# Row sums of the adaLN blocks: one group of matmuls for up to four blocks

## The chip, the cores and the metric

The kernel runs on one core of a Trainium2 chip. Its engines work side by side, each through its own list of instructions: TensorE (PE, with its weight loads as PEld) multiplies matrices, VectorE (DVE), ScalarE (ACT) and GpSimd (POOL) work on elements, and SyncE (SP) issues the DMA transfers. SBUF is the working memory, PSUM holds what TensorE writes, in eight banks. The metric is the device time of one execution in microseconds. The kernel before took 2109.31 us in the median of 3 runs (2108.45 to 2116.08).

## The reference

A backbone of two layers works on 256 latent and 256 context tokens of 1024 features. Each layer is a feed-forward part, a token mixing of four branches, and a second feed-forward part. Before each of them the tokens are normalised, scaled and shifted, and its result is gated. These nine vectors of a layer come from the conditioning alone:

```python
mod = [m[:, None, :] for m in jnp.split(jax.nn.silu(c) @ w_ada[l] + b_ada[l], N_MOD, axis=-1)]
mod_c = jnp.split(jax.nn.silu(c_ctx) @ w_ada[l] + b_ada[l], N_MOD, axis=-1)

def ffn_half(z, shift, scale, gate, norm, wg, wu, wd):
    return z + 0.5 * gate * swiglu(modulate(rmsnorm(z, norm), shift, scale), wg, wu, wd)
```

`w_ada[l]` has 1024 rows and 9 x 1024 columns. There are only two rows of conditioning (c and c_ctx), so this product is a very thin one: two output rows, 9216 columns, for each layer.

## The kernel before

**The main stream.** The tokens lie in SBUF with features on the 128 partitions. Every large product is made with split operands: a weight unit of 128 x 1024 is brought in (`raw`), ScalarE rounds it to `whi` (line 81), VectorE takes the rest as `wlo` (line 84), and TensorE makes three matmuls of 512 columns for each of 8 steps (lines 110 to 112): 24 products to a unit. In a feed-forward part the units come in pairs, `pg` (gate) and `pu` (up), then the down products `pd`, and for the last two chunks `last`. Their results go through three PSUM banks in turn (`mm`); four further banks are for small things and one, `ada`, for the work of this change. The weights have four buffers for `whi` and four for `wlo`, so ScalarE and VectorE work up to four units ahead.

**The adaLN blocks.** The thin product is cut into 18 blocks of 512 columns for each layer. The first four blocks of layer 0 are made on TensorE at the cold start (`ada_pe`, line 263, 32 columns of weights in each of four column tiles). The other 14 of layer 0 and all 18 of layer 1 are worked off beside the feed-forward stream by a generator, `ada` (line 274). For a block, VectorE multiplies each of the four pieces of weights (512 KB each) with the conditioning and adds them into two accumulators `aacc` (lines 283 and 285), one for c and one for c_ctx. At the end of a block the 128 partitions have to be summed: two copies on ScalarE and two additions on VectorE fold both accumulators into one tile `afold`, its upper half for c and its lower half for c_ctx (lines 292 to 295). Then TensorE sums the rows of each half: the weights are `pick`, 128 x 32, with a one in column 0 or 1, and four matmuls of 128 columns go to four column tiles, that is to four groups of 32 partitions of the bank (line 297). `ada_done` reads the bank with one 32 x 32-wise transpose (line 250, tile `adat`) and adds the biases in two small additions (line 253), whose results stand in `mod`.

**What sets the order.** `pump` advances the generator by one step; `unit` calls it after each weight unit, at a rate. A block has four steps, with one piece of weights each. `mods` pumps until the values that a stage needs are there. At the end of a feed-forward part (`f == 1`) the open block is finished before the last chunks begin, in layer 0's first part and layer 1's first part all that are left. The engines' lists are made from this code by a scheduler, which keeps TensorE's work in the order of the code and may move element work a little.

The names that the prediction uses: `afold` (the folded block), `ada` (its PSUM bank), `adat` and `mod` (its read-out), `whi`/`wlo` (weights), `pg`, `pu`, `pd` (PSUM results), `sg` (the Silu of `pg`, line 535).

Of the kernel before, what the change touches and what calls it, by code (L numbers as in the profile page):

```python
# [10 lines left out]
F32 = mybir.dt.float32  # L11
# [6 lines left out]
P = 128  # L18
# [4 lines left out]
TT = 2 * T  # L23
# [9 lines left out]

RATE_FIRST, RATE_NEXT = 1.0, 0.62


O_AQ, O_AK, O_AV, O_BQ, O_BF, O_BB, O_BI, O_BG, O_C, O_DQ, O_DK, O_DV, O_G = (
    0, 256, 384, 512, 768, 1024, 1280, 1536, 1792, 2048, 2304, 2560, 2816)
# [20 lines left out]
class Net:  # L59
    def __init__(self, ctx, tc, ins, out):  # L60
        self.ctx, self.tc, self.nc, self.i, self.out = ctx, tc, tc.nc, ins, out
        self.n = 0
        pool = lambda name, **kw: ctx.enter_context(tc.tile_pool(name=name, **kw))
        self.cp = pool("const", bufs=1)
        self.wp = pool("weights", bufs=4)
        self.tp = pool("temps", bufs=2)
        self.ps = pool("psum", bufs=1, space=bass.MemoryType.PSUM)
        self.fill = self.apool = None
        self.steady, self.due = False, 0.0


# [197 lines left out]
    def ada(self, l, first):  # L269


        nc = self.nc
        for s in range(first, 18):
            self.within = True
            acc = [self.apool.tile([P, 512], F32, tag=f"aacc{r}", name="aacc") for r in range(2)]
            for k2 in range(NK // 2):
                w = self.ada_load(l, s, k2)
                for j in range(2):
                    k = 2 * k2 + j
                    for r in range(2):  # L280
                        c = self.sil[:, k, r:r + 1]
                        if k == 0:
                            nc.vector.tensor_scalar(out=acc[r], in0=w[:, j], scalar1=c, scalar2=None, op0=ALU.mult)
                        else:
                            nc.vector.scalar_tensor_tensor(out=acc[r], in0=w[:, j], scalar=c, in1=acc[r],  # L285
                                                           op0=ALU.mult, op1=ALU.add)
                if k2 < NK // 2 - 1:
                    yield True
            ps = self.ps.tile([P, TT], F32, tag="ada", bufs=1, name="ada")

            t = self.apool.tile([P, 512], F32, tag="afold", name="afold")
            nc.scalar.copy(t[:64], acc[0][64:])
            nc.scalar.copy(t[64:], acc[1][:64])
            nc.vector.tensor_tensor(out=t[:64], in0=t[:64], in1=acc[0][:64], op=ALU.add)
            nc.vector.tensor_tensor(out=t[64:], in0=t[64:], in1=acc[1][64:], op=ALU.add)
            for g in range(4):
                nc.tensor.matmul(ps[32 * g:32 * g + 32, :P], self.pick, t[:, g * P:(g + 1) * P], start=True, stop=True,
                                 tile_position=(0, 32 * g))
            self.ada_done(l, s, ps)
            self.within = False  # L300
            yield True

    def mods(self, l, j):
        while not set(range(j * NK, (j + 1) * NK)) <= self.have[l]:
            assert self.fill
            self.pump()
        return self.mod[l][:, j * NK:(j + 1) * NK]

    def gain(self, l, j, col):
# [162 lines left out]
    def cold_units(self, wgu, hp, evac, off):  # L472
# [32 lines left out]
        for _ in ada(0):  # L505
            pass
        self.keep_warm(8)
        ws = [self.unit(wgu[u // 2, u % 2]) for u in range(4)]
        aw += [loads(j) for j in range(1, 4)]
        steps = chain.from_iterable(ada(j) for j in range(1, 4))  # L510
        for item in COLD:
            if item == "a":
# [8 lines left out]
        return hh, hl  # L521

    def ffn(self, l, wgu, wd, col, mods, segs, rate=0, whole=False, cold=False):

        nc, tc = self.nc, self.tc
        n = T * len(segs)
        gate = None
        off = self.place(l, col)
        with tc.tile_pool(name=f"ffn{col}_{l}", bufs=1) as hp:
            hp.tile([P, LINE // 2], F32, name="pad")  # L530
            self.apool, self.rate = hp, rate
            def evac(pg, pu, hh, hl, c, c0, c1):
                w = c1 - c0
                s = hp.tile([P, TT], F32, tag="sg", bufs=2, name="sg")
                nc.scalar.activation(s[:, :w], pg[:, :w], AF.Silu)
                nc.vector.tensor_tensor(out=s[:, :w], in0=s[:, :w], in1=pu[:, :w], op=ALU.mult)
                self.split(s[:, :w], hh[:, c, c0:c1], hl[:, c, c0:c1])

            for f in range(2):
                c = 0  # L540
                if cold and f == 0:
                    hh, hl = self.cold_units(wgu[l], hp, evac, off)
                    c = 2
                    self.steady = True
                else:
                    hh, hl = self.hidden(hp, off)
                while c < FH:
                    if f == 0 and c == 0:
                        def first(r, j0, pss):
                            for j in range(0, len(pss), 2):  # L550
                                evac(pss[j], pss[j + 1], hh, hl, c + (j0 + j) // 2, *HALF[r])

                        ws = [self.unit(wgu[l, c + j // 2, j % 2]) for j in range(4)]
                        if len(segs) == 1:
                            self.early_units(ws, l, hp, hh, hl)
                        else:
                            self.first_units(ws, l, col, mods[0], mods[1], segs, lambda r: (
                                [self.mm(), self.mm(), self.mm(), self.aux()] if r == 0 else
                                [self.aux(), self.aux(), self.mm(), self.mm()]), first, 2)
                        c += 2  # L560
                        self.steady = True
                        continue
                    pg, pu = self.mm("pg"), self.mm("pu")
                    pool = hp if f == 0 and c == 2 else None
                    for j, p in ((0, pg), (1, pu)):
                        self.mm3(p[:, :n], self.unit(wgu[l, f * FH + c, j], NK * P, pool), self.xh, self.xl, range(NK), 0, n)
                    evac(pg, pu, hh, hl, c, 0, n)
                    c += 1
                if gate is None:
                    gate = self.gate(l, mods[2])  # L570
                if f == 1:
                    self.fresh(segs)

                def down(m, ps, c0, c1, mid=iter(()), ws=[None] * NK):
                    if ws[m] is None:
                        pool = hp if f == 1 and m >= NK - 2 else None
                        ws[m] = (self.unit(wd[l, f, m, :, :6 * P], 6 * P, pool),
                                 self.unit(wd[l, f, m, :, 6 * P:], (FH - 6) * P, pool))
                    self.mm3(ps, ws[m][0], hh, hl, range(6), c0, c1, last=False)
                    next(mid, None)  # L580
                    self.mm3(ps, ws[m][1], hh, hl, range(6, 9), c0, c1, first=False, last=False)
                    next(mid, None)
                    self.mm3(ps, ws[m][1], hh, hl, range(9, FH), c0, c1, first=False, k0=3)

                for m in range(NK - 2 * f):
                    ps = self.mm("pd")
                    down(m, ps[:, :n], 0, n)
                    for r in segs:
                        self.update(ps, m, gate, r, r * T, f == 1)
                if f == 1:  # L590
                    while self.fill and (whole or self.within):
                        self.pump()
                    self.steady = False
                    self.last_chunks(down, gate, segs)

# [659 lines left out]
```

## Time and profile before

| | us |
|---|---|
| median of 3 runs | 2109.31 |
| lowest and highest | 2108.45, 2116.08 |
| the profiled execution | 2115.61 |
| its span, first to last instruction | 2113.8 |
| TensorE busy in it | 2087.5 (99%) |
| VectorE busy | 1434.9 (68%) |
| ScalarE busy | 904.5 (43%) |

The span is the profiled execution from its first to its last instruction; 1.8 us lie around it. A busy share is an average over stages. Matmuls overlap one another, and their ends are modelled, so a matmul's duration is not what it costs: that is read from the starts of the instructions before and after it. TensorE's granted clock is at its upper level, 2.4 GHz, in all slices of the page.

### The profile page before, as it was taken

How to read it: one execution, taken by the hardware profiler on the slowest of the kernel's cores; microseconds unless marked ns; L12 is line 12 of the kernel's file. 1: busy time of each engine (PE TensorE's matmuls, PEld its weight loads, DVE VectorE, ACT ScalarE, POOL GpSimd, SP SyncE). 2: the span in 40 equal slices, each digit the busy share in tenths (PEclk: the TensorE clock that was granted, in tenths of full speed). 3: DMA queues.
4: the chain of work that ended last, by engine and by line, in shares of the span. 5: the costliest groups of instructions: out<-in, count | busy, mean ns of one | idle time of the engine just before them, and what ended most of it. 6: DMA issues, size and time to landing. Idle time of an engine off the chain costs nothing.

```text
span 2113.8 us, 31650 instructions
## 1 busy us (share of the span) xinstructions
PE 2087.5 (99%) x12446; PEld 1801.0 (85%) x12446; DVE 1434.9 (68%) x2355; ACT 904.5 (43%) x1488; POOL 39.4 (2%) x95
## 2 busy tenths in 40 slices
PE   8999999999999999999999999999999999999998
PEld 5888888988888888988888898888889989999998
DVE  5988986676366455676676667667666858677555
ACT  3332333547446433433233343223335655666443
POOL 0000000001000000000000000000000000000000
PEclk9999999999999999999999999999999999999999
DMA  7655654221222222344454334345443233455553
GB/s 304 216 175 188 215 186 140 96 98 51 75 76 80 71 97 98 110 143 138 144 183 157 124 128 161 130 156 173 146 128 114 98 120 110 141 184 181 176 189 116
DMA packets 89509, 296.71 MB, mean 140 GB/s; under 512 B 10256, under 2 KB 12176, under 8 KB 89360
## 3 DMA queue, kind: packets, MB, share of 16 engines
q1 hardware_dynamic: 89360, 294.69, 41.4%
q8 instruction: 98, 1.61, 0.3%
q14 instruction: 51, 0.42, 0.1%
HBM read 293.60 MB, written 1.05 MB: 139 GB/s over the span
## 4 chain that ended last, share of the span: by engine, by line
PE 94%; DVE 2%; ACT 2%; issue 1%; DMA 0%; DVEq 0%; ACTq 0%; SPq 0%
PE pg L110 6%; PE pu L110 6%; PE pg L112 6%; PE pu L112 6%; PE pg L111 6%; PE pu L111 6%; PE pd L110 6%; PE pd L112 6%; PE pd L111 6%; PE gate L112 4%; PE gate L110 4%; PE gate L111 4%; PE proj L111 2%; PE proj L110 2%; PE proj L112 2%; PE blev L777 2%
## 5 line engine op out<-in xcount | busy, mean ns | idle before, releaser
L81 ACT CAST whi<-raw 128x1024 fp32r<-128x1024 f32 (+2 forms) x444 | 430.7, 972 | 827.4 <-PE pu L111 200.3
L84 DVE TENSOR_TENSOR wlo<-raw,whi 128x1024 fp32r<-128x1024 f32 (+2 forms) x444 | 498.2, 1123 | 289.3 <-ACT whi L81 282.5
L285 DVE SCALAR_TENSOR_TENSOR aacc<-araw,sil,aacc 128x512 f32<-128x512 f32 x448 | 312.5, 745 | 122.0 <-DMA araw<-in_wada 121.6
L112 PE MATMUL pg<-xs,wlo 128*128 128x512 f32 (+1 forms) x640 | 233.0, 364 | 0.0
L112 PE MATMUL pu<-xs,wlo 128*128 128x512 f32 (+1 forms) x640 | 233.0, 364 | 0.0
L110 PE MATMUL pg<-xs,whi 128*128 128x512 f32 (+1 forms) x640 | 232.5, 363 | 0.4 <-ACT xs L376 0.4
L110 PE MATMUL pu<-xs,whi 128*128 128x512 f32 (+1 forms) x640 | 232.3, 363 | 0.0
L111 PE MATMUL pg<-xs,whi 128*128 128x512 f32 (+1 forms) x640 | 231.4, 362 | 0.0
L111 PE MATMUL pu<-xs,whi 128*128 128x512 f32 (+1 forms) x640 | 231.3, 361 | 0.0
L112 PE MATMUL pd<-hh,wlo 128*128 128x512 f32 (+1 forms) x616 | 224.3, 364 | 0.0
L110 PE MATMUL pd<-hh,whi 128*128 128x512 f32 (+1 forms) x616 | 223.8, 363 | 0.0
L111 PE MATMUL pd<-hl,whi 128*128 128x512 f32 (+1 forms) x616 | 222.7, 361 | 0.0
L110 PE MATMUL gate<-xs,whi 128*128 128x512 f32 (+1 forms) x512 | 172.5, 337 | 0.0
L112 PE MATMUL gate<-xs,wlo 128*128 128x512 f32 (+1 forms) x512 | 171.7, 335 | 0.0
L111 PE MATMUL gate<-xs,whi 128*128 128x512 f32 (+1 forms) x512 | 170.8, 334 | 0.0
L110 PEld LDWEIGHTS pg<-xs,whi 128*128 128x128 f32 x640 | 120.8, 189 | 20.8 <-issue 1.8
L110 PEld LDWEIGHTS pu<-xs,whi 128*128 128x128 f32 x640 | 120.8, 189 | 20.1 <-issue 2.0
L111 PEld LDWEIGHTS pu<-xs,whi 128*128 128x128 f32 x640 | 120.2, 188 | 19.4
L111 PEld LDWEIGHTS pg<-xs,whi 128*128 128x128 f32 x640 | 120.2, 188 | 19.4
L112 PEld LDWEIGHTS pg<-xs,wlo 128*128 128x128 f32 x640 | 120.1, 188 | 18.5
L112 PEld LDWEIGHTS pu<-xs,wlo 128*128 128x128 f32 x640 | 120.1, 188 | 18.5
L110 PEld LDWEIGHTS pd<-hh,whi 128*128 128x128 f32 x616 | 116.2, 189 | 19.5 <-issue 2.2
(278 smaller groups left out, 3794.5 us busy)
## 6 DMA issues: line engine op xcount, KB each, us to landing
raw<-in_wgu SPq DMA_DIRECT2D x176, 512.0 KB, 4.0
araw<-in_wada SPq DMA_DIRECT2D x128, 512.0 KB, 3.3
raw<-in_wgate SPq DMA_DIRECT2D x64, 512.0 KB, 3.2
raw<-in_wd SPq DMA_DIRECT2D x64, 384.0 KB, 3.1
raw<-in_win SPq DMA_DIRECT2D x44, 512.0 KB, 3.3
raw<-in_wd SPq DMA_DIRECT2D x64, 320.0 KB, 2.8
aspace<-in_wada SPq DMA_DIRECT2D x16, 512.0 KB, 8.9
raw<-in_wbr SPq DMA_DIRECT2D x16, 512.0 KB, 3.3
```

The costliest lines, as they stand in the source:

```text
L81: nc.scalar.copy(hi, src)
L84: nc.vector.tensor_tensor(out=lo, in0=src, in1=hi.bitcast(F32), op=ALU.subtract)
L110: nc.tensor.matmul(ps, wh, a, start=first and j == 0, stop=False)
L111: nc.tensor.matmul(ps, wh, b, start=False, stop=False)
L112: nc.tensor.matmul(ps, wl, a, start=False, stop=last and j == n - 1)
L285: nc.vector.scalar_tensor_tensor(out=acc[r], in0=w[:, j], scalar=c, in1=acc[r], op0=ALU.mult, op1=ALU.add)
L777: nc.tensor.matmul(ps[:, g * P:(g + 1) * P], k[:, h, g * P:(g + 1) * P], x[:, h, (g ^ cross) * P:((g ^ cross) + 1) * P], start=True, stop= ...
```

## The change

The generator keeps each finished `afold` (in four buffers now) in a list, `sums`. When four blocks are in it, or at a layer's last block (18 blocks a layer, s == 17), or when `flush` is set, `fold` makes the matmuls of all of them in a row, each block into its own 128 columns of the one bank, and then reads them out one after the other. `flush` is set while `mods` pumps for values that are not there yet, and at the end of a feed-forward part.

```diff
+        sums = []
+
+        def fold():
+
+            ps = self.ps.tile([P, TT], F32, tag="ada", bufs=1, name="ada")
+            for j, (s, t) in enumerate(sums):
+                for g in range(4):
+                    nc.tensor.matmul(ps[32 * g:32 * g + 32, j * P:(j + 1) * P], self.pick, t[:, g * P:(g + 1) * P],
+                                     start=True, stop=True, tile_position=(0, 32 * g))
+            for j, (s, t) in enumerate(sums):
+                self.ada_done(l, s, ps[:, j * P:(j + 1) * P])
+            sums.clear()
+            self.within = False
+
         for s in range(first, 18):
+            if sums and self.flush:
+                fold()
+                yield True
             self.within = True
...
-            ps = self.ps.tile([P, TT], F32, tag="ada", bufs=1, name="ada")
-
-            t = self.apool.tile([P, 512], F32, tag="afold", name="afold")
+
+            t = self.apool.tile([P, 512], F32, tag="afold", bufs=FOLD, name="afold")
...
-            for g in range(4):
-                nc.tensor.matmul(ps[32 * g:32 * g + 32, :P], self.pick, t[:, g * P:(g + 1) * P], start=True, stop=True,
-                                 tile_position=(0, 32 * g))
-            self.ada_done(l, s, ps)
-            self.within = False
+            sums.append((s, t))
+            if len(sums) == FOLD or s == 17 or self.flush:
+                fold()
             yield True
 
     def mods(self, l, j):
         while not set(range(j * NK, (j + 1) * NK)) <= self.have[l]:
             assert self.fill
+            self.flush = True
             self.pump()
+        self.flush = False
...
                 if f == 1:
+                    self.flush = True
                     while self.fill and (whole or self.within):
                         self.pump()
+                    self.flush = False
```

FOLD is 4.

On TensorE, at the end of the fourth block (in layer 0's first feed-forward part, between the products of a `pg` and of its `pu`), the order before was:

```order
L112 MATMUL pg<-xs,wlo 128x512
L297 MATMUL ada<-afold,pick 32x128 x4
L110 MATMUL pu<-xs,whi 128x512
L111 MATMUL pu<-xs,whi 128x512
L112 MATMUL pu<-xs,wlo 128x512
```

At the same place it is now:

```order
L115 MATMUL pg<-xs,wlo 128x512
L283 MATMUL ada<-afold,pick 32x128 x16
L113 MATMUL pu<-xs,whi 128x512
L114 MATMUL pu<-xs,whi 128x512
L115 MATMUL pu<-xs,wlo 128x512
```

The matmuls of the first three blocks have moved here from their own places, 288, 192 and 96 products of the stream earlier; what stands before and behind is the same.

On VectorE, the read-out of that fourth block stood so (`adat` is the transpose, `mod_92` the values of layer 0):

```order
L285 SCALAR_TENSOR_TENSOR aacc<-araw,sil,aacc 128x512 x4
L250 STREAM_TRANSPOSE adat<-ada 128x128
L84 TENSOR_TENSOR wlo<-raw,whi 128x768
L253 TENSOR_TENSOR mod_92<-adat,cols_70 128x4 x2
L285 SCALAR_TENSOR_TENSOR aacc<-araw,sil,aacc 128x512 x4
```

It is now, for the first four blocks:

```order
L87 TENSOR_TENSOR wlo<-raw,whi 128x768
L253 STREAM_TRANSPOSE adat<-ada 128x128 x2
L256 TENSOR_TENSOR mod_92<-adat,cols_70 128x4 x4
L253 STREAM_TRANSPOSE adat<-ada 128x128 x2
L256 TENSOR_TENSOR mod_92<-adat,cols_70 128x4 x4
L337 TENSOR_SCALAR gate<-mod_92 128x16
L305 SCALAR_TENSOR_TENSOR aacc<-araw,sil,aacc 128x512 x4
```

Four read-outs stand behind one another, the gate that waits for them directly behind, and the next accumulations after that.

On ScalarE, a little earlier in the same part, the order before was:

```order
L81 CAST hh<-sg 128x512
L81 CAST whi<-raw 128x1024
L535 ACTIVATE sg<-pg 128x512
L292 COPY afold<-aacc 64x512
L293 COPY afold<-aacc 64x512
```

It is now:

```order
L84 CAST hh<-sg 128x512
L311 COPY afold<-aacc 64x512
L554 ACTIVATE sg<-pg 128x512
L312 COPY afold<-aacc 64x512
L84 CAST whi<-raw 128x1024 x2
```

The first copy has moved ahead of the Silu that empties a gate bank; at three later places both copies have.

## Rows read from the trace of the kernel before

**Rows 1.** The page: span, busy time, tenths in 40 slices, the chain's shares.
```profile
span 2113.8 us, 31650 instructions
...
PE 2087.5 (99%) x12446; PEld 1801.0 (85%) x12446; DVE 1434.9 (68%) x2355; ACT 904.5 (43%) x1488; POOL 39.4 (2%) x95
...
DVE  5988986676366455676676667667666858677555
...
PE 94%; DVE 2%; ACT 2%; issue 1%; DMA 0%; DVEq 0%; ACTq 0%; SPq 0%
```

**Rows 2.** Timeline, TensorE around one block's matmuls: start us, us, engine, line, operation.
```profile
272.64 0.39 PE L112 MATMUL pu<-xs,wlo 128*128 128x512 f32 x1
272.96 0.42 PE L297 MATMUL ada<-afold,pick 128*32 128x128 f32 x8
273.31 0.50 PE L110 MATMUL pg<-xs,whi 128*128 128x512 f32 x1
273.65 0.39 PE L111 MATMUL pg<-xs,whi 128*128 128x512 f32 x1
```

**Rows 3.** Busy time in one stretch (records in brackets), and timeline of two products.
```profile
93.49:115.88 22.39, 22.39 (x105) 18.11 (x104) 21.79 (x35) 7.61 (x10) 0.00 (x0) 1.00 0.69 231
...
256.55 0.39 PE L110 MATMUL pu<-xs,whi 128*128 128x512 f32 x1
...
261.99 0.39 PE L110 MATMUL pg<-xs,whi 128*128 128x512 f32 x1
```

**Rows 4.** Timeline, TensorE at the cold start, around two runs of line 263.
```profile
37.17 0.39 PE L125 MATMUL mm<-xs,whi 128*128 128x512 f32 x1
37.49 0.65 PE L263 MATMUL ada<-aspace,sil 128*32 128x128 f32 x16
38.06 0.50 PE L123 MATMUL mm<-xs,whi 128*128 128x512 f32 x1
...
40.00 0.39 PE L125 MATMUL aux<-xs,whi 128*128 128x512 f32 x1
40.32 1.52 PE L263 MATMUL ada<-aspace,sil 128*32 128x128 f32 x48
41.76 0.50 PE L123 MATMUL mm<-xs,whi 128*128 128x512 f32 x1
```

**Rows 5.** Tiles afold and adat: durations in ns (min/median/max), waits before them.
```profile
L297 PE MATMUL ada<-afold,pick x256: 272/285/297, 71.4 to 1581.2; 128*32 128x128 f32 x128
...
L253 DVE TENSOR_TENSOR mod<-adat,cols x72: 148/154/165, 18.4 to 1584.5; 128x4 f32<-128x4 f32 x72
L250 DVE STREAM_TRANSPOSE adat<-ada x36: 253/308/317, 18.1 to 1583.3; 128x128 f32<-128x128 f32 x36
...
  PE ada L297: 0.8, 2
```

**Rows 6.** Timeline, VectorE at the fourth block's read-out, and TensorE's first product from that wlo.
```profile
139.09 0.32 DVE L250 STREAM_TRANSPOSE adat<-ada 128x128 f32<-128x128 f32 x1 [0.26 <-PE ada L297]
139.39 0.96 DVE L84 TENSOR_TENSOR wlo<-raw,whi 128x768 fp32r<-128x768 f32 x1
140.26 0.23 DVE L253 TENSOR_TENSOR mod<-adat,cols 128x4 f32<-128x4 f32 x2
...
155.91 0.39 PE L112 MATMUL pd<-hh,wlo 128*128 128x512 f32 x1
```

**Rows 7.** Waits of ScalarE and TensorE: total us, times, longest us.
```profile
ACT whi L81 <- PE pu L111: 200.3, 66, 4.7
...
PE mm L123 <- ACT whi L81: 0.9, 1, 0.9
```

**Rows 8.** Timeline, ScalarE: a Silu, and a block's first copy with its wait.
```profile
139.26 0.59 ACT L535 ACTIVATE sg<-pg 128x512 f32<-128x512 f32 x1
...
144.25 0.62 ACT L292 COPY afold<-aacc 64x512 f32<-64x512 f32 x1 [4.40 <-DVE aacc L285]
```

More of the change, by code (lines that the diff above doesn't have):

```diff
@@ L34 @@
 RATE_FIRST, RATE_NEXT = 1.0, 0.62
+FOLD = 4
 O_AQ, O_AK, O_AV, O_BQ, O_BF, O_BB, O_BI, O_BG, O_C, O_DQ, O_DK, O_DV, O_G = (
@@ L590, in ffn @@
                 if f == 1:
+                    self.flush = True
                     while self.fill and (whole or self.within):
                         self.pump()
+                    self.flush = False
                     self.steady = False
```

## The prediction

> **What bounds the kernel now.** I read the page first. TensorE is busy 99% of the span and 94% of the chain that ended last is TensorE's own instructions [rows 1]; no other engine has more than 2% of it. So only what shortens TensorE's instruction stream, or makes it wait, can change the time. The VectorE slices matter as a warning: from the second to the sixth slice (about 53 to 317 us, where layer 0's blocks are worked off) it reads 8 or 9 tenths, then mostly 5 to 7 [rows 1].
>
> Next I read the timeline of TensorE around one block's row sums, called a visit here. The products of the main stream start 0.227 us apart; between the last one before the visit (272.64) and the first one after it (273.31) lie 0.67 us, and the next start is 0.34 us later still [rows 2]. The visit holds 8 records: four matmuls in four column tiles, each two records. The gap alone does not give the whole price, since the stream is uneven for some products after it. For that I took a stretch from one visit to the next: 22.39 us with 105 records, which are 96 products, 8 of a visit and the one at the edge [rows 3]. 24 products without a visit take 261.99 - 256.55 = 5.44 us [rows 3], 0.2267 each, so 96 take 21.76 and one visit costs 22.39 - 21.76 = 0.63 us all told, the unevenness included.
>
> **What the change removes.** Thirty-two blocks (14 of layer 0, 18 of layer 1) make 32 visits now, 32 x 0.63 = 20.2 us on TensorE's path. The order of the changed kernel has ten: of 16 matmuls seven times, of 8 once, of 4 twice (14 = 4+4+4+2; layer 1's 18 = 4+4+1 before the end of layer 0's second feed-forward, 4+4+1 in layer 1's first). No matmul is dropped: 128 before and after. Apart from the folds TensorE's order is the same row for row, and so are SyncE's and GpSimd's; the tiles keep their addresses but for the three further afold buffers. So the sum is about 22 sets of four matmuls that no longer open a visit of their own, but stand behind another set.
>
> **What such a set costs behind another.** The trace before has no run of more than one afold set, but it has the same form of matmul (128*32 weights, 128 columns, f32, four column tiles) in longer runs at the cold start, and there the same stream stands on both sides [rows 4]. Sixteen records (two sets): from the last product before to the first after 38.06 - 37.17 = 0.89 us. Forty-eight records (six sets): 41.76 - 40.00 = 1.76 us. Four further sets cost 0.87 us, 0.2175 each. The one set of rows 2 fits on that line: 0.67 + 0.22 = 0.89. The durations agree too: 285 ns is the median of a record in the visits [rows 5], and the records overlap.
>
> So a moved set costs 0.2175 instead of 0.63, and 22 of them save 22 x (0.63 - 0.2175) = 9.1 us. The bounds: if a set of the new runs cost as much as the bare gap of a visit less one product's pitch, 0.67 - 0.23 = 0.44, the saving would be 22 x 0.19 = 4.2 us; if it cost a whole visit, nothing. If further sets were free it would be 22 x 0.63 = 13.9 us. I take 0.2175, since rows 4 are the same instruction in the same place between the same products, and keep 4.2 and 13.9 for the range.
>
> **What moves, at no cost.** Three things.
> First, VectorE's read-out. A block has one transpose (0.308 us) and two additions (0.154 each) [rows 5], 0.62 us; four blocks now have them in one burst of 4 x 0.62 = 2.46 us, and the weight halves (wlo) queued behind it come up to 1.85 us later. What hides it: the weights are made ahead of their use. The wlo that stands beside the fourth block's transpose was made at 139.39 [rows 6], and the first product that reads it starts at 155.91 [rows 6], a lead of 15.6 us after its end. ScalarE's casts wait for TensorE to free a buffer (200.3 us for pu alone) and TensorE's list of waits has only one for a weight cast, of 0.9 us [rows 7], on a product of the cold start. The transposes themselves wait for the run, which is 0.65 us longer than a visit; VectorE stood 0.8 us in two waits for it so far [rows 5], and it is idle for 32% of the span [rows 1]. Without that lead each burst would stand on the path; that is the third rival.
> Here a page of the Trainium skill speaks against the change. The Trainium skill (TensorEngine Tiling, Performance Considerations, "PSUM Bottleneck") says that column tiling speeds up TensorE but not the emptying of PSUM, which may become the bottleneck, and advises reading several tiles of one bank with one instruction; this kernel keeps four transposes for the four blocks. By that rule the read-out would decide the time and the sum would be the third rival's; by rows 6 and 7 it decides nothing, and the sum stays at 9.1.
> Second, ScalarE's order. At four places the Silu that empties a gate bank now stands behind one or both copies of a block's accumulators; such a copy waits for VectorE's accumulation, at the longest 4.40 us [rows 8]. That wait, two copies of 0.62 and a Silu of 0.59 [rows 8] make 6.2 us. The bank is wanted again after two more units of 24 products, 2 x 5.44 = 10.9 us. So nothing reaches TensorE.
> Third, the modulation values come later by up to three blocks. The gate of layer 0's first feed-forward is made from the first fold, at about 141 us by the place of the fourth block's transpose [rows 6]; it is wanted by the first update from pd, whose product group is just beginning at 155.91 [rows 6]. The last fold before the tail of layer 0's second feed-forward moves to the first `last` product; its read-out is 0.62 us on VectorE before an update that has a whole group of products to wait for.
>
> **The sum.** The profiled execution has a span of 2113.8 and 2115.61 us in all; less 9.1 it would be 2106.5. The median of the runs shown is 2109.31, 6.3 below it; the executions lie in two groups, 2108.45 and 2109.31, and 2115.61 and 2116.08. From the median: 2109.3 - 9.1 = **2100.2 us**, 0.43% faster, which is within the 0.5% that a measurement of this kernel can just tell from no change.
>
> **Rivals.**
> A set in the new runs is dearer than in rows 4. For it: there the four sets accumulate into one place in PSUM, here each set begins its own quarter of the bank with its own data. Against it: the visits' entry and records are like those of rows 4. At 0.44 a set: 2109.3 - 4.2 = 2105.1 us.
> The visits hid more than 0.63. For it: the slowed stream after a visit; free sets would give 2109.3 - 13.9 = 2095.4, and half way, 2097.8, is already beyond 0.5%. Against it: rows 4 put a price on the further sets.
> The bursts take the path. VectorE's burst delays wlo, TensorE stands at the next unit. The price is the whole read-out: 7 x 2.46 + 1.23 + 2 x 0.62 = 19.7 us, less 9.1: 2109.3 + 10.6 = 2119.9 us, slower. It decides from the point where the lead of wlo at a fold is below 2.5 us. For it: VectorE near its full share in the early slices [rows 1]. Against it: the lead of 15.6 us.
> That the change folds block by block after all, because of the flush flag, is ruled out by the order's ten runs.
>
> **How the numbers follow.** The forecast (a set at 0.2175, a saving of 8 to 10) has a chance of 0.70; the dearer set 0.13; the larger saving 0.13; the bursts 0.04. Range: if the median falls in the upper group of executions, 2116 - 9.1 = 2107, and the dearer set gives 2105, so the upper end is 2107.8. The lower end is 2097.5, just past the half-way case of the larger saving. Faster by over 0.5% (below 2098.8) is the larger saving and a little of the forecast's scatter, 0.15; slower by over 0.5% is the bursts, 0.04; the rest, 0.81, lies between.
>
> **What would show it.** Ten groups of afold matmuls; about 1.33 us (0.67 + 3 x 0.22) from the last product before a run of 16 to the first after it, 0.67 at the two single ones; the other 22 places with products 0.227 apart; a stretch of 96 products without a fold in 21.76 us; TensorE's waits no longer than before; a span 9 us shorter. Wrong would be: a gap of more than 1.6 us at a run of 16 (the dearer set), TensorE waiting for wlo or whi behind a fold (the bursts), or visits gone and the span unchanged, which would mean that TensorE's stream is not what sets the time.

## The result, and the profile after

| | us | ratio to before |
|---|---|---|
| before, median of 4 runs | 2109.63 (2108.45 to 2116.08) | |
| after, median of 4 runs | 2099.72 (2099.07 to 2099.82) | 0.995 (0.9937 to 0.9963) |
| forecast | 2100.2 (2097.5 to 2107.8) | |

The change makes the kernel 9.9 us faster in the medians, 0.47%: the interval of the ratio leaves out 1, and the change is within the 0.5% that the forecast named.

The page of the profile after, the lines that answer to [rows 1]:

```profile
span 2097.8 us, 31638 instructions
...
PE 2072.1 (99%) x12446; PEld 1798.3 (86%) x12446; DVE 1434.9 (68%) x2355; ACT 906.3 (43%) x1488; POOL 39.5 (2%) x95
...
PE 93%; DVE 3%; ACT 2%; issue 1%; DMA 0%; DVEq 0%; ACTq 0%; SPq 0%
```

Each engine has the same number of records as before, VectorE the same busy time, and TensorE is still 93% of the chain. The span is 16.0 us shorter, 6.1 more than the medians are apart; what makes up the rest is settled below.

The timeline of TensorE at the first run of 16 matmuls answers to [rows 2] (32 records are 16 matmuls; line 283 is the fold, 113 to 115 the products):

```profile
136.32 0.39 PE L115 MATMUL pg<-xs,wlo 128*128 128x512 f32 x1
136.65 1.08 PE L283 MATMUL ada<-afold,pick 128*32 128x128 f32 x32
137.66 0.50 PE L113 MATMUL pu<-xs,whi 128*128 128x512 f32 x1
138.00 0.40 PE L114 MATMUL pu<-xs,whi 128*128 128x512 f32 x1
```

From the last product before the run to the first one after it lie 1.34 us; the forecast had 1.33. The entry (0.33 us from that product to the first record of the run) and the 0.34 us behind the first product are those of a single visit, and the three further sets cost 0.22 each. A stretch that held a visit before has none now (busy time in one stretch, records in brackets, against [rows 3]):

```profile
93.49:115.25 21.76, 21.76 (x98) 18.02 (x97) 21.64 (x32) 7.70 (x11) 0.00 (x0) 1.00 0.71 237
```

Of the 98 records two overlap the edges; the other 96 are products, and 21.76 us is their length, as forecast. Summed from the last product before it to the twelfth behind it, less twelve pitches of 0.2267 us, a run of four sets costs 1.23 us, the run of two sets 0.78, a single one 0.63 (the forecast summed over 96 products; over 90 the figures are the same). The forecast's 0.63 + 3 x 0.2175 would be 1.28. The difference lies behind the run: there the stream loses a further 0.18 us behind a single set, 0.13 behind four and 0.11 behind two. So the ten runs take 7 x 1.23 + 0.78 + 2 x 0.63 = 10.7 us, the 32 visits took 20.3, and the saving on TensorE is 9.6 us where 9.1 was forecast.

VectorE's read-out and TensorE's waits, against [rows 5] and [rows 7] (first tile adat, then a line of TensorE's waits: total us, times, longest):

```profile
L256 DVE TENSOR_TENSOR mod<-adat,cols x72: 118/155/165, 18.4 to 1575.0; 128x4 f32<-128x4 f32 x72
L253 DVE STREAM_TRANSPOSE adat<-ada x36: 253/307/318, 18.1 to 1573.8; 128x128 f32<-128x128 f32 x36
...
  PE ada L266: 10.5, 3
```
```profile
PE mm L126 <- ACT whi L84: 0.8, 1, 0.8
```

The only wait of the read-out that is left is the one for the cold start's matmuls (line 266); the 0.8 us for the row sums are gone, though the runs are longer. TensorE waits for no weight half behind a fold: the one wait for `whi` is that of the cold start, which was there before.

### The profile page after: what moved, and what is told of

The parts are those of the page before. It is cut to its first block, busy times and chain, and to the rows that moved or that the text cites. A ratio compares the mean times of both kernels' runs of the same rounds, so it can differ in the third digit from the quotient of the medians.

```text
span 2097.8 us, 31638 instructions
## 1 busy us (share of the span) xinstructions
PE 2072.1 (99%) x12446; PEld 1798.3 (86%) x12446; DVE 1434.9 (68%) x2355; ACT 906.3 (43%) x1488; POOL 39.5 (2%) x95
## 4 chain that ended last, share of the span: by engine, by line
PE 93%; DVE 3%; ACT 2%; issue 1%; DMA 0%; DVEq 0%; ACTq 0%; SPq 0%
PE pg L115 6%; PE pu L115 6%; PE pg L113 6%; PE pu L113 6%; PE pu L114 6%; PE pg L114 6%; PE pd L115 6%; PE pd L113 6%; PE pd L114 6%; PE gate L115 4%; PE gate L113 4%; PE gate L114 4%; PE proj L114 2%; PE proj L115 2%; PE proj L113 2%; PE blev L798 2%
## 5 line engine op out<-in xcount | busy, mean ns | idle before, releaser
L114 PEld LDWEIGHTS pd<-hl,whi 128*128 128x128 f32 x616 | 115.6, 188 | 18.6
```

The costliest lines, as they stand in the source:

```text
L114: nc.tensor.matmul(ps, wh, b, start=False, stop=False)
```

## The experiments

**The kernel before, once more.** No edit.

> The kernel before, unchanged. Its profiled execution has a span 16.0 us longer than that of the kernel after, but the medians differ by 9.9 us and the visits on TensorE by 9.6. The other 6.4 us lie in the last feed-forward part, where the 256-column products start 117.8 ns apart before and 113.3 after. Theory: these are two states of the same code, unrelated to the change, and they make the two groups of executions (about 2109 and 2116). Then an execution of about 2109 has 113.3 ns there and one of about 2116 has 117.8. Rival: the change itself brought 113.3; then every execution of the kernel before has 117.8 whatever its time. Ratio 1.000 within 0.3%.

Measured: 2115.34 us median of 10 runs: four between 2108.1 and 2109.2, six between 2115.0 and 2115.8. The kernel before beside it had 35 runs: 15 between 2108.2 and 2110.3, 20 between 2115.0 and 2116.9. So there are two groups, their medians 6.5 us apart, and nothing between them. In the stretch from 2000 to 2050 us, which lies in the last feed-forward part, the number of TensorE's records tells the pitch, the time from the start of one product to the start of the next (first the profile of before that the forecast rests on, an execution of 2115.61; then the one after, 2099.71):

```profile
2000.00:2050.00 50.00, 50.00 (x427) 50.00 (x426) 28.85 (x35) 24.11 (x34) 0.00 (x0) 1.00 0.61 206
```
```profile
2000.00:2050.00 50.00, 50.00 (x444) 50.00 (x443) 28.88 (x36) 24.99 (x38) 0.00 (x0) 1.00 0.58 190
```

Less two records that overlap the edges, these are 425 products of 256 columns against 442 in 50 us; by their starts they are 117.8 and 113.3 ns apart, at the same granted clock (the 1.00 in both rows). The profiled execution here (2115.76) has 117.8; the ones of the next experiments fit too: 2107.74 (two blocks to a run) with 117.8, 2109.89 (grouped read-out alone) and 2099.19 (the longer burst) with 113.3. The part has some 1,490 such products (40 units of 24 and 16 groups of 33); at 4.45 ns each these are 6.6 us, the distance between the groups. The theory holds. Its rival falls by the 2109.89, though that is not the unchanged kernel, of which no execution near 2109 was profiled. The nearest is the kernel before with one extra matmul (below): its part runs at 113.3 from the sixth product on, before that matmul comes.

**After, once more.** No edit.

> The kernel after, unchanged, to see whether it has the two groups too. Theory (the pitch of the last feed-forward part is drawn anew in each execution, whatever the kernel): a lower group at 2099 to 2100 and an upper one at 2106 to 2107, each 9.6 us below the same group of the kernel before. Rival (the change fixes the pitch at 113.3): all executions at 2099 to 2100.

Measured: five runs between 2098.2 and 2100.5, three between 2106.2 and 2106.9; the kernel before beside it 14 between 2107.8 and 2110.5, nine between 2115.0 and 2115.9. The profiled execution, of the upper group (2106.25), has the longer pitch:

```profile
2000.00:2050.00 50.00, 50.00 (x427) 50.00 (x426) 28.65 (x36) 23.89 (x35) 0.00 (x0) 1.00 0.62 193
```

The change does not touch the pitch. Group by group it is worth 9.8 us (medians of the lower groups 2099.5 and 2109.3) and 9.2 (of the upper groups 2106.4 and 2115.6). The four runs of the result were all of the lower group.

**Two blocks to a run.**

```diff
-FOLD = 4
+FOLD = 2
```

> Two blocks to a run instead of four: 17 runs, 15 of 8 matmuls and 2 of 4. Theory (a run costs a fixed part and a set of four matmuls about 0.2 us): by the runs of the kernel after, 0.63 us for one set, 0.78 for two: 15 x 0.78 + 2 x 0.63 = 13.0 us against 20.3 before, so 7.3 us faster than before, about 2102.3. Rival (the saving comes from the grouped read-out on VectorE, in proportion to how many stand together): half of the saving or less, about 2105.

Measured: three runs between 2101.1 and 2102.2, nine between 2107.7 and 2108.9. Between the medians of the lower groups, 2101.6 against 2109.4, it is 7.8 us; of the upper groups, 2108.6 against 2115.8, 7.2. The theory said 7.3, the rival half of the saving or less; the theory holds. One of the 15 double visits:

```profile
92.41 0.39 PE L115 MATMUL pg<-xs,wlo 128*128 128x512 f32 x1
92.73 0.64 PE L283 MATMUL ada<-afold,pick 128*32 128x128 f32 x16
93.30 0.50 PE L113 MATMUL pu<-xs,whi 128*128 128x512 f32 x1
```

From product to product 0.89 us, as at the cold start's pair in [rows 4]. Half the grouping brings some three quarters of the gain: it takes away 15 of the 32 visits, the whole grouping 22.

**Grouped read-out alone.** The matmuls stay at their 32 places; only the read-out waits for four blocks (`add` makes a block's matmuls at once, `fold` now has the read-outs alone).

```diff
+        def add(s, t):
+
+            if not sums:
+                banks[:] = [self.ps.tile([P, TT], F32, tag="ada", bufs=1, name="ada")]
+            j = len(sums)
+            for g in range(4):
+                nc.tensor.matmul(banks[0][32 * g:32 * g + 32, j * P:(j + 1) * P], self.pick, t[:, g * P:(g + 1) * P],
+                                 start=True, stop=True, tile_position=(0, 32 * g))
+            sums.append((s, t))
...
-            sums.append((s, t))
+            add(s, t)
             if len(sums) == FOLD or s == 17 or self.flush:
                 fold()
```

> The matmuls block by block as before (32 visits of four), each block into its own 128 columns of one bank; only the read-outs are grouped by four as after. Theory (the fixed part of a visit on TensorE is the whole gain): 32 x 0.63 us, no change, 2109 to 2110. Rival (the grouped read-out brings it): as after, about 2100. Rival of the bursts (the grouped read-out costs): above 2112.

Measured: four runs between 2108.7 and 2109.9, eight between 2114.7 and 2116.9, ratio 1.0003 (0.999 to 1.0016). There is no gain and no loss: VectorE's grouping neither brings the gain nor costs. With the 32 visits back (each 0.63 us by its trace, 0.68 from product to product) the whole saving is gone, so it was TensorE's.

**The burst, eight times as long.** The read-outs of a fold are done eight times over.

```diff
-            for j, (s, t) in enumerate(sums):
-                self.ada_done(l, s, ps[:, j * P:(j + 1) * P])
+            for _ in range(8):
+                for j, (s, t) in enumerate(sums):
+                    self.ada_done(l, s, ps[:, j * P:(j + 1) * P])
```

> The kernel after, with all read-outs of a fold done eight times in a row: the burst of a run of 16 is 8 x 2.46 = 19.7 us of VectorE instead of 2.46. Theory (the weights' lead of some 15 us hides a burst): TensorE stands only for what exceeds the lead, 2 to 8 us at each of seven bursts, 2110 to 2150. Rival (bursts stand on the path): 7 x 17.2 + 8.6 + 2 x 4.3 = 138 us more, about 2238. If the lead were even longer: 2100.

Measured: 2099.19 and nine runs between 2104.7 and 2107.0, the groups of the kernel after. The burst costs nothing, and its size was wrong in my expectation. VectorE's timeline, first and last rows of the burst of the first fold and the next weight half:

```profile
138.86 0.51 DVE L253 STREAM_TRANSPOSE adat<-ada 128x128 f32<-128x128 f32 x2
139.29 0.35 DVE L256 TENSOR_TENSOR mod<-adat,cols 128x4 f32<-128x4 f32 x4
...
149.69 0.35 DVE L256 TENSOR_TENSOR mod<-adat,cols 128x4 f32<-128x4 f32 x4
...
150.63 0.82 DVE L87 TENSOR_TENSOR wlo<-raw,whi 128x640 fp32r<-128x640 f32 x1
```

Eight read-outs of four blocks take 11.2 us, 1.4 us each, not 2.46: instructions that follow one another overlap here (two transposes of 0.31 us stand in 0.51), and durations added up overstate them. Even 11.2 us stay within the lead of 15.6 [rows 6], and TensorE's list of waits has no entry for a weight but the cold start's. Where the lead ends was not reached.

**Without column tiles.** From the kernel before: the weights are 128 x 128 with zeros, and the four matmuls add up in one place.

```diff
+            wide = self.apool.tile([P, 7 * 32], F32, tag="wide", name="wide")
...
-                nc.tensor.matmul(ps[32 * g:32 * g + 32, :P], self.pick, t[:, g * P:(g + 1) * P], start=True, stop=True,
-                                 tile_position=(0, 32 * g))
+                nc.tensor.matmul(ps[:, :P], wide[:, 96 - 32 * g:224 - 32 * g], t[:, g * P:(g + 1) * P],
+                                 start=g == 0, stop=g == 3)
```

> The kernel before, block by block, but the row sums without column tiles: four f32 matmuls with 128 x 128 weights (zeros but for two columns) that accumulate into one place; the results are the same. Eight records of 128 columns at full width stand 112 ns apart at the cold start (the warm matmuls), so 0.89 us to a block. Theory A (the fixed part of a visit comes from changing the column tiles): no fixed part here, 0.9 to 1.0 us a visit, 32 x 0.3 = 10 us slower than before. Theory B (it comes from changing between the rounded and the full f32 kind of matmul): 0.4 + 0.89 = 1.3 us a visit, 21 us slower.

Measured: four runs between 2118.3 and 2119.8, two at 2124.7 and 2125.3: 9.9 us above before in the lower group (medians 2119.2 and 2109.3), of which the visits make 9.0, 0.28 each. A visit:

```profile
94.04 0.39 PE L112 MATMUL pg<-xs,wlo 128*128 128x512 f32 x1
94.28 1.05 PE L301 MATMUL ada<-afold,wide 128*128 128x128 f32 x8
95.08 0.48 PE L110 MATMUL pu<-xs,whi 128*128 128x512 f32 x1
```

The entry takes 0.24 us, hardly more than the stream's 0.227, against 0.32 with column tiles [rows 2]. Summed over twelve products as above, the visit costs 0.91 us; its eight records, 0.1115 us apart, are 0.89 of it. Theory A holds: the fixed 0.4 us of a visit comes with the column tiles and is gone without them. Theory B, the other kind of f32, falls: the kind still changes here.

**Without tiles and in the rounded kind.** As the last, with `afold` and the weights rounded like the stream's operands.

```diff
-            t = self.apool.tile([P, 512], F32, tag="afold", name="afold")
+            t = self.apool.tile([P, 512], F32R, tag="afold", name="afold")
...
+            wider = self.apool.tile([P, 7 * 32], F32R, tag="wider", name="wider")
+            nc.gpsimd.tensor_copy(wider, wide)
...
+                nc.tensor.matmul(ps[:, :P], wider[:, 96 - 32 * g:224 - 32 * g], t[:, g * P:(g + 1) * P],
+                                 start=g == 0, stop=g == 3)
```

> As the last, with folded block and weights in the rounded f32 kind that the main stream has (this rounds the row sums): neither tiles nor kind change in a visit. Theory A and theory B: no fixed part, four records only, 0.25 to 0.5 us a visit, 4 to 12 us faster than before. If the fixed part of 0.4 us stays, it is neither of the two, but short products in a stream of long ones: 0.65 to 0.9 us a visit.

Measured: 2107.59 us median of 8 runs (2105.3 to 2108.2), ratio 0.9977 (0.9964 to 0.999). By its trace a visit has four records and 0.62 us from product to product (94.06 to 94.68, for one); summed over twelve products it costs 0.53 us, and the 32 together 3.4 us less than before. The expected 0.25 to 0.5 us a visit and 4 to 12 us in all were both missed. Three records of 128 columns take 0.11 us each, as long as the 256-column products of the last part; with the fourth that makes 0.45 us, and about 0.08 us are left beside the records, which neither theory accounts for. Three runs lie between 2105.3 and 2105.8, where 3.4 us less than the lower group of before would be, and five between 2107.5 and 2108.2; the profiled one (2108.19) has 113.3 ns in the last part, so these two clusters are not the groups of above. What sets them apart is open.

**Five blocks to a run.** Two banks for a run, `FOLD = 5`.

```diff
-FOLD = 4
+FOLD = 5
...
-            ps = self.ps.tile([P, TT], F32, tag="ada", bufs=1, name="ada")
+            ps = [self.ps.tile([P, TT], F32, tag="ada", bufs=1, name="ada")]
+            if len(sums) > 4:
+                ps.append(self.aux("ada"))
...
```

> Five blocks to a run instead of four, in two banks: layer 0 in 5+5+4, layer 1 in 5+4 and 5+4, seven runs in place of ten, no single sets. Theory: a run costs about 0.42 and a set 0.2, so 3 x 0.42 = 1.3 us faster than the kernel after, group by group: 2098 and 2105. Rival (the second bank delays the small matmuls of a stage): 2100 or more in the lower group.

Measured: five runs between 2098.1 and 2100.6, one at 2105.9. Against the kernel after (2098.2 to 2100.5) this shows nothing; the groups' own scatter of 2 us is too wide for the 1.3 us expected. The last experiment has it again without the groups.

**Four extra matmuls in the last feed-forward part.**

```diff
                     pg, pu = self.mm("pg"), self.mm("pu")
+                    if len(segs) == 1 and c in (4, 8):
+                        self.keep_warm(1)
```

> The kernel after, with one extra f32 matmul (128 x 128 ones, 128 columns, results unused) before four pairs of units in the last feed-forward part, where the 256-column products run at 113.3 or at 117.8 ns for the whole part. Theory (the pitch is a state that the stream keeps until something breaks it): at some of the four places the pitch changes, and the times fill the range between 2100 and 2108 instead of two groups. Rival (the pitch is fixed for an execution by something outside the stream): one pitch over the whole part, two groups 6.5 us apart, about 1 us above those of the kernel after.

Measured: 2099.8 to 2101.5 in 5 runs, one group. One of the four had been moved ahead of that part by the scheduler, to 1854.6 us of the profiled execution, so that not every matmul stays in the order of the code; the first that stands in it is at 1951.2. Two stretches of 25 us, before and behind it:

```profile
1920.00:1945.00 25.00, 25.00 (x215) 25.00 (x214) 16.71 (x23) 13.36 (x22) 0.00 (x0) 1.00 0.64 207
1955.00:1980.00 25.00, 25.00 (x223) 25.00 (x222) 14.28 (x21) 11.05 (x18) 0.00 (x0) 1.00 0.54 157
```

213 products against 221: the pitch goes from 117.8 to 113.3 ns in one execution, at one matmul, and stays to the end, past two more such matmuls. So it is not fixed from outside. The expected spread up to 2108 did not come. That the pitch might be drawn anew at each such matmul, five runs do not rule out; the next experiments were made for that.

**One extra matmul, in three kernels.** One f32 matmul of 128 columns after the first 48 products of the part, on the tile `rstd` so that it stays there; in the kernel after, before, and with five blocks to a run.

```diff
+                    if len(segs) == 1 and f == 0 and c == 3:
+                        ps = self.ps.tile([P, TT], F32, tag="ada", bufs=1, name="nudge")
+                        nc.tensor.matmul(ps[:, :P], self.ones, self.rstd[0][:, :P], start=True, stop=True)
```

> The kernel after, with one extra f32 matmul (128 x 128 ones, 128 columns of the tile rstd, result unused) in the last feed-forward part, after its first 48 products. In the run with four such matmuls the pitch went from 117.8 to 113.3 ns at the first one that stood in that part, and stayed. Theory (a matmul of another kind brings the stream to 113.3): one group, 2098.5 to 2100.7. Rival (it draws the pitch anew): two groups as before, 2099 to 2100.7 and 2106 to 2107.2.

> The same one matmul in the kernel before. Theory: one group, 2108 to 2110.3; with the run before it in this call the change is then read free of the two groups, as 9.6 us. Rival: two groups, 2108 and 2115.

> Five blocks to a run, and the same one matmul. Theory: one group, 0.9 us below the kernel after with that matmul (seven runs of 1.51 or 1.23 us make 9.7 us, ten made 10.7), 2097.6 to 2099.8. Rival: no difference, since the runs' groups scatter by 2 us.

| with the one matmul | runs | median us | lowest, highest | ratio to before |
|---|---|---|---|---|
| after | 5 | 2099.53 | 2098.99, 2100.65 | 0.9934 (0.9919 to 0.9948) |
| before | 11 | 2109.30 | 2108.28, 2110.66 | 0.9979 (0.997 to 0.9988) |
| five blocks to a run | 5 | 2098.54 | 2097.69, 2098.99 | 0.9927 (0.9914 to 0.9939) |

The kernel before beside them, without it: five runs below 2110, ten above 2114.7. With it none of 21 runs is in an upper group, so the pitch is not drawn anew: the theory holds in all three. The profile of the kernel after, in 4.8 us ahead of the one matmul and 4.8 us behind it:

```profile
1918.50:1923.30 4.80, 4.80 (x43) 4.80 (x42) 4.73 (x9) 4.79 (x7) 0.00 (x0) 1.00 0.34 116
1925.00:1929.80 4.80, 4.80 (x45) 4.80 (x44) 3.20 (x6) 2.38 (x5) 0.00 (x0) 1.00 0.69 218
```

By the starts of the products the pitch is 117.8 ns ahead of the matmul and 113.3 behind it, and so it is in the profile with five blocks; the kernel before was at 113.3 on both sides.

Free of the groups the change is worth 2109.30 - 2099.53 = 9.8 us, and five blocks to a run another 1.0 us, where the traces said 0.9 to 1.0 (ten runs 10.7 us, seven runs 9.7). The version with five blocks and the one matmul has the lowest median of all that were tried. By its trace a run of five sets has 1.55 us from product to product (152.61 to 154.16, for one) and costs 1.51 over the twelve products behind it, so that behind the run 0.18 us are lost, as much as behind a single set.

## Why the prediction was right

**What bounds the kernel**: right. TensorE's stream was the whole account: its visits take 9.6 us less, and the time, free of the groups, is 9.8 us less.

**The visits**: right, 0.63 us each, 32 before and ten runs after, of the sizes that the order gave. The grouped read-out alone, with the 32 visits kept, gave nothing.

**The price of a set behind another**: right in mechanism and within 0.01 us, from rows of another line with the same form. The size that was off is the unevenness after a run: the forecast kept a single visit's 0.18 us, and it is 0.13 behind four sets and 0.11 behind two. Seven times 0.05 and the 0.07 of the double run are most of the 0.5 us between 9.1 and 9.6; the rest is rounding (a visit is 0.633). It does not shrink with the length of the run, since behind five sets it is 0.18 again; what it depends on is open.

**What a visit's fixed part is** the forecast did not say. It comes with the column tiles: with tiles 0.63 us for a set whose further copies cost 0.22, so 0.41 fixed; without tiles 0.91 us for records that alone take 0.89, so 0.02. The Trainium skill (TensorEngine Tiling (Array Packing), Tiling Modes, "Key Properties") says that changing the tiling mode drains TensorE. These runs agree as far as they go: the 0.41 us are there where the mode changes and gone where it does not; that a drain is what takes them, no run shows.

**VectorE's burst**: rightly put at nothing, but the price in reserve was too high. Four read-outs in a row take 1.4 us, not 2.46, and the slower rival's 19.7 us would have been about 11. The Trainium skill (TensorEngine Tiling (Array Packing), Performance Considerations, "PSUM Bottleneck") says that emptying PSUM may become the bottleneck. Here it did not: apart from the cold start VectorE's read-out has neither waited nor been waited for, and eight times as much of it cost nothing.

**ScalarE's moved copies and the later modulation values**: rightly put at nothing; TensorE has no wait behind them that it did not have before.

**The dearer set and the larger saving** as rivals: the first falls by the 1.34 us gap (its sign was a gap of more than 1.6); of the second a tenth is there, 0.5 of 4.8 us.

**The two groups**: the forecast saw them in four numbers, did not know their cause, and gave the range its upper end for them. That was needed: three of eight later runs of the kernel after came out at 2106 to 2107. That the result fell within 0.5 us of the forecast was in part luck: the median that the forecast started from was of the lower group, and so were all four runs of the result. The 9.6 us of the change do not depend on it. The profiled execution before was of the upper group and the one after of the lower; the 6.6 us between the groups are what their spans differ beyond the change (16.0 - 9.6 = 6.4).

## What to carry to other kernels

A short job on TensorE is priced by what the stream around it loses, from one product to the next and on until the pitch is steady again, not by its own duration. Where it needs column tiles in a stream that has none, count the excursions, whose fixed part was 0.4 us each here, and gather what can wait into one. And where executions fall into two groups, compare within a group, or find what sets the groups apart, before two profiles are subtracted.

## What had not been expected of the hardware

The same 256-column products ran at 117.8 or at 113.3 ns, over a whole part of some 170 us and some 1,490 products, with the granted clock at its full level in both. Which of the two an execution gets is settled within the first few products of the part, in the kernel before nearly as often one as the other (46 runs below 2111 us, 49 above 2114). One f32 matmul of 128 columns, on full width, in the middle of the stream brought 117.8 to 113.3 in each of the three profiled executions that had 117.8 before it, and no run out of 26 with such a matmul took the upper time. At 113.3 it changed nothing. Whether its kind of f32 or its number of columns does it was not tried.

The last part is not the only place. In the token mixing of layer 1, ten microseconds near its end read so in two profiles of the unchanged kernel before, the forecast's and the one taken again, both with 117.8 ns in the last part:

```profile
1896.00:1906.00 10.00, 10.00 (x91) 10.00 (x90) 9.45 (x16) 8.49 (x14) 0.00 (x0) 1.00 0.61 216
```
```profile
1896.00:1906.00 10.00, 10.00 (x87) 10.00 (x86) 8.89 (x14) 7.89 (x12) 0.00 (x0) 1.00 0.63 206
```

By their starts these products stand 113.3 and 117.8 ns apart. So a stretch can have one pitch and the next the other, and some of the 2 us by which runs of one group scatter may come from there; how much was not measured. Why the stream has two pitches, and what that one matmul resets, is open; the 512-column products showed one pitch alone, 226.7 ns, wherever the visits were measured.
